# Three small edits to the edges of a TensorE-bound kernel: the order of the last products, 256-column matmuls in the first set, and the place of the branch hints

## The chip, the cores and the metric

One core of a Trainium2 chip. The time is the device time of one execution in microseconds (us). A trace was taken of one execution of each kernel; every other execution has only its time and its span.

Engine names: PE is TensorE's matmuls, PEld its weight loads, DVE VectorE, ACT ScalarE, POOL GpSimd, SP SyncE; SPq is DMA issue on SyncE. L250 is a line of the kernel of that run.

## The reference

```python
# x: 16 x 256 x 512, w1: 512 x 4096, w2: 2048 x 512, all float32
h = x @ w1
gate, value = np.split(h, 2, axis=-1)
h = np.maximum(gate, 0) * value
out = (h @ w2).astype(np.float32)
```

## The kernel before

Both matrix products are done with a seven-product scheme on 2x2 blocks (P1 to P7 instead of eight products), in float16, over four sets of 1024 rows. A first matmul runs through blocks of 128 hidden units (class `Block`, 128x512 outputs); a second one through four "pairs" of row blocks for each set (class `Pair`, 128x256 outputs). Each product of a pair ends in a small operation on ScalarE or VectorE and, in some cases, in a send of the output by SyncE.

The order of the products of the last set's second matmul is a list; the number is that of the pair:

```python
ORDER = ("P1 0, P1 1, P2 0, P2 1, P1 2, P5 0, P2 2, P6 0, P3 0, P7 0, P5 1, P6 1, P3 1, P7 1, P4 0, P5 2, P4 1, "
         "P6 2, P3 2, P7 2, P1 3, P4 2, P5 3, P2 3, P6 3, P3 3, P7 3, P4 3")
...
LAST_ORDER = ORDER.replace("P5 3, P2 3, P6 3, P3 3, P7 3", "P2 3, P6 3, P5 3, P7 3, P3 3")
# so it ends: P7 2, P1 3, P4 2, P2 3, P6 3, P5 3, P7 3, P3 3, P4 3
```

P6, P7 and P4 of a pair add into the same PSUM tile `Y`, and VectorE reads `Y` after P7 and before P4:

```python
def P7(self):
    nc.vector.scalar_tensor_tensor(out=self.o[:, 1, DO // 2:], in0=self.Y, scalar=1 / GS, in1=self.pu[:, 0],
                                   op0=MULT, op1=ADD)
    if self.end:
        self.send(1, slice(DO // 2, DO))

def P4(self):
    nc.scalar.activation(self.o[:, 1, :DO // 2], self.Y, COPY, scale=1 / GS)
    self.send(1, slice(0, DO // 2 if self.end else DO))
```

The scheme needs inputs of ordinary size, so the kernel checks its inputs while it works. A branch at the end leads to a plain general way if the check failed, and over it (some 3,360 TensorE instructions) if not. Hints for that branch are placed by one job of the last second matmul:

```python
with tc.If(unfit > 0, label="general"):
    ...            # general_way: not run with these inputs
...
job(84, lambda: tc.mark_branch_hint_location("general", "LikelyTaken", [ENG.PE, ENG.DVE, ENG.SP]))
```

Although this job is traced near the end, the built program has the three hint instructions at the very start of TensorE's, VectorE's and SyncE's programs. In the trace they start at 0.82, 0.77 and 0.74 us and take 0.05 to 0.06 us each.

Of the kernel before, what the change touches and what calls it, by code (L numbers as in the profile page):

```python
# [9 lines left out]
F32, F32R, F16 = dt.float32, dt.float32r, dt.float16  # L10
# [4 lines left out]
ENG = mybir.EngineType  # L15

P = 128
TH = 512
# [8 lines left out]
@with_exitstack  # L27
def kernel(ctx: ExitStack, tc: tile.TileContext, x, w1, w2, out):






    nc = tc.nc
    x2 = x.flatten_outer_dims()
    out2 = out.flatten_outer_dims()
    flagpool = ctx.enter_context(tc.tile_pool(name="flagpool", bufs=1))
    flag = flagpool.tile([1, 1], dt.int32, name="flag")
    with ExitStack() as fast:  # L40
        unfit = fast_way(fast, tc, x2, w1, w2, out2, flag)
    with tc.If(unfit > 0, label="general"):
        with ExitStack() as general:
            general_way(general, tc, x2, w1, w2, out2)
# [52 lines left out]
def fast_way(ctx, tc, x2, w1, w2, out2, flag):  # L97
# [9 lines left out]
    nc = tc.nc  # L107
    T, D = x2.shape
    _, J = w1.shape
    H, DO = w2.shape  # L110
    NS = T // (2 * TH)
    NJ = H // P
    NB = 2 * TH // P

    ctx.enter_context(tc.manual_schedule(engines={ENG.PE, ENG.DVE, ENG.Activation, ENG.Pool, ENG.SP}))
    wpool = ctx.enter_context(tc.tile_pool(name="wpool", bufs=1))
    xpool = ctx.enter_context(tc.tile_pool(name="xpool", bufs=2))
    gpool = ctx.enter_context(tc.tile_pool(name="gpool", bufs=1))
# [2 lines left out]
    tmp = ctx.enter_context(tc.tile_pool(name="tmp", bufs=6))  # L121
# [9 lines left out]
    wop = {n: wpool.tile([P, 2, H], F16, name=f"w_{n}") for n in ("B11", "B21", "B22", "T1", "T2", "T3", "T4")}  # L131
# [26 lines left out]
    def x_tiles():  # L158

        o = {n: xpool.tile([P, 2, TH], F16, name=f"x_{n}", tag=f"x_{n}")  # L160
             for n in ("A11", "A12", "A22", "S1", "S2", "S3", "S4")}
        o["A21"] = o["S3"]
        return o
# [3 lines left out]
    def sum_of(o, n, eng=nc.vector):  # L167
        i0, i1, op = SUMS_X[n]
        eng.tensor_tensor(o[n], o[i0], o[i1], op=op)  # L169

    def sums_of(o, eng=nc.vector):
        for n in SUMS_X:
            yield sum_of(o, n, eng)
# [67 lines left out]
          "P5": ("T1", "S1"), "P6": ("T2", "S2"), "P7": ("T3", "S3")}  # L241

    class Block:
        def __init__(self, xo, g, jb):
            self.xo, self.g, self.jb, self.behind = xo, g, jb, ()

        def mm(self, name, ps, fresh):
            wn, xn = WX[name]
            for b in range(2):
                nc.tensor.matmul(ps, wop[wn][:, b, self.jb * P:(self.jb + 1) * P], self.xo[xn][:, b, :],  # L250
                                 start=fresh and b == 0, stop=b == 1, skip_group_check=True)

        def P1(self):
            self.X = psx.tile([P, TH], F32, name="X", tag="X")
# [11 lines left out]
        def P2(self):  # L266
            self.mm("P2", self.X, False)
# [17 lines left out]
        def P7(self):  # L285
            self.mm("P7", self.Y, False)
            nc.vector.scalar_tensor_tensor(out=self.c22, in0=self.Y, scalar=GS, in1=self.p5, op0=MULT, op1=ADD)  # L287
            for job in self.behind:
                job()
            second_halves()  # L290
# [13 lines left out]
    def second_halves():  # L304

        while later:
            later.pop(0).second_half()
# [34 lines left out]

    class Pair:
        def __init__(self, s, g, t):
            self.s, self.t = s, t
            self.end = s == NS - 1 and t != NB // 2 - 2
            o = {f"A{h + 1}{u + 1}": g[:, u * NJ // 2:(u + 1) * NJ // 2, h * TH + t * P:h * TH + (t + 1) * P]
                 for h in range(2) for u in range(2)}
            o.update({f"S{n + 1}": s_place[:, t % 2, n] for n in range(4)})
            self.op = o  # L350

        def product(self, name):
# [8 lines left out]
            for i in range(NJ // 2):  # L361
# [4 lines left out]
                if i % 2:  # L366
                    yield

        def send(self, h, c):
            nc.sync.dma_start(out=out_v[self.s, h, self.t, :, c], in_=self.o[:, h, c])  # L370

# [8 lines left out]
                some_look()  # L380

        def P2(self):
            self.o = tmp.tile([P, 2, DO], F32, name="o", tag="tmp")
            nc.scalar.activation(self.o[:, 0, :DO // 2], self.X, COPY, scale=1 / GS)
            if self.end:
                self.send(0, slice(0, DO // 2))
# [9 lines left out]
            self.send(0, slice(DO // 2 if self.end else 0, DO))  # L396

        def P7(self):
            nc.vector.scalar_tensor_tensor(out=self.o[:, 1, DO // 2:], in0=self.Y, scalar=1 / GS, in1=self.pu[:, 0],
                                           op0=MULT, op1=ADD)  # L400
            if self.end:
# [5 lines that stand above are left out]
            if self.t in ((0, 2) if self.s else (0, 1, 2)):  # L407
                some_look()

    ORDER = ("P1 0, P1 1, P2 0, P2 1, P1 2, P5 0, P2 2, P6 0, P3 0, P7 0, P5 1, P6 1, P3 1, P7 1, P4 0, P5 2, P4 1, "  # L410
             "P6 2, P3 2, P7 2, P1 3, P4 2, P5 3, P2 3, P6 3, P3 3, P7 3, P4 3")
    FIRST_ORDER = ("P1 0, P1 1, P2 0, P2 1, P1 2, P5 0, P2 2, P6 0, P3 0, P5 1, P6 1, P3 1, P5 2, P6 2, P3 2, P7 0, P7 1, "
                   "P4 0, P7 2, P4 1, P1 3, P4 2, P5 3, P2 3, P6 3, P3 3, P7 3, P4 3")
    LAST_ORDER = ORDER.replace("P5 3, P2 3, P6 3, P3 3, P7 3", "P2 3, P6 3, P5 3, P7 3, P3 3")

    def mm2_stream(s, pairs):
        for step in (LAST_ORDER if s == NS - 1 else ORDER if s else FIRST_ORDER).split(", "):
            name, t = step.split()
            yield from pairs[int(t)].product(name)
# [3 lines left out]
    def advance(stream, n, todo={}):  # L423

        for _ in range(n):
            if stream is None:
                return
            at = stream_at[stream] = stream_at.get(stream, -1) + 1
            for job in todo.get(at, ()):
                job()  # L430
            next(stream, 0)
# [45 lines left out]
    g = g_set[0]  # L477
    x_nat = x2.rearrange("(s h b p) d -> s h b p d", h=2, b=4, p=P)
    place = [*x_tiles().values()][:7] + [halfs.tile([P, 8, P], F16, name="xh", tag="xh")]
    xn = [[t.rearrange("p a b -> p (a b)").bitcast(F32) for t in place[4 * h:4 * h + 4]] for h in range(2)]  # L480
# [3 lines left out]
    half, other = (0, TH // 2), (TH // 2, TH)  # L484
# [42 lines left out]
    xo = x_tiles()  # L527
# [53 lines left out]
    sums = [{n: t[:, :, slice(*c)] for n, t in xo.items()} for c in (half, other)]  # L581
# [54 lines left out]
    def judge():  # L636
        n = st.shape[1]
        ok = wpool.tile([P, n], F32, name="ok")
        fit = wpool.tile([P, 2], F16, name="fit")
        nc.vector.tensor_scalar(out=ok, in0=st, scalar1=HIGH, scalar2=None, op0=LE)  # L640
        nc.vector.scalar_tensor_tensor(out=ok, in0=st, scalar=LOW, in1=ok, op0=GE, op1=MULT)
        nc.vector.memset(fit, 1.0)
        with nc.allow_low_precision("whole numbers below 2048"):
            nc.vector.tensor_reduce(out=fit[:, :1], in_=ok, axis=mybir.AxisListType.X, op=ADD)
        return fit

    def count(fit):
        n = P * st.shape[1]
        ps = psx.tile([P, TH], F32, name="X", tag="X")
        nc.tensor.matmul(ps[:1, :1], fit[:, :1], fit[:, 1:], start=True, stop=True)  # L650
        nc.vector.tensor_scalar(out=flag, in0=ps[:1, :1], scalar1=n - 0.5, scalar2=None, op0=LT)
# [14 lines left out]
    for s in range(NS):  # L666
        if s not in g_set:
            g_set[s] = gpool.tile([P, NJ, 2 * TH], F16, name="g", tag="g")
        g = g_set[s]
        first = NPLAIN if s == 0 else 0  # L670
        blocks = {jb: Block(xo, g, jb) for jb in range(first, NJ)}
        plan = {jb * PERIOD + at: (jb, n) for jb in blocks for n, at in SLOT.items()}
        if s == 0:
            for n in ("P5", "P2", "P3"):
# [6 lines left out]
        last = NJ * PERIOD  # L681
        todo = 3
        for at in range(first * PERIOD, (NJ - 1) * PERIOD + 14):
            if at == last - 7:
                pairs = [Pair(s, g, t) for t in range(NB // 2)]
                stream = mm2_stream(s, pairs)
            if at in plan:
                jb, n = plan[at]
# [17 lines left out]
                if s and n == "P3" and jb in SUMS and s + 1 < NS:  # L706
                    if jb == SUMS[0]:
                        sums = sums_of(xo_next, nc.gpsimd)
# [18 lines left out]
        def job(at, *what):  # L727
            jobs.setdefault(at, []).extend(what)

        for t, at in enumerate(SUMS_AT if s else SUMS_FIRST):  # L730
            sums = sums_of(pairs[t].op)
            for u in at:
                job(u, lambda sums=sums: next(sums))
        if s == 0:
# [6 lines left out]
        if s + 1 < NS:  # L741
            xo = xo_next
            if s == 0:
                sums = sums_of(xo)
                for u in (84, 90):
                    job(u, lambda sums=sums: next(sums))
            looks = [lambda i=i: LOOK_JOBS[i]() for i in range(8 * s, 8 * s + 8)]
            advance(stream, 112 - TAIL - 10, jobs)
            if s == 0:
                next(sums)  # L750
                next(sums)
        else:
            verdict = []
            job(18, lambda: verdict.append(judge()))
            job(46, lambda: count(verdict[0]))
            job(78, lambda: verdict.append(nc.values_load(
                flag[0:1, 0:1], min_val=0, max_val=1, skip_runtime_bounds_check_because="a comparison wrote it")))
            job(84, lambda: tc.mark_branch_hint_location("general", "LikelyTaken", [ENG.PE, ENG.DVE, ENG.SP]))
            advance(stream, 112, jobs)
        prev = stream  # L760
    return verdict[-1]
# [28 lines left out]
```

## Time and profile before

| | before |
|---|---|
| time, median of the three runs known when the prediction was made | 308.57 us |
| span of the traced execution | 307.16 us |
| PE busy | 301.6 us, 98% |
| first matmul's wait, and the last wait on loads | 1.3 us; up to 18.7 us |
| start of the last matmul to the end ("the tail" below) | 4.40 us |

From the page of the kernel before: the span, the first of the busy times (us, share of the span, instructions), and the start of its part 4, the chain of work that ended last.

```profile
span 307.2 us, 5283 instructions
...
PE 301.6 (98%) x1905; PEld 184.2 (60%) x1905; DVE 236.0 (77%) x388; ACT 176.3 (57%) x348; POOL 151.2 (49%) x189
...
PE 96%; DMA 2%; SPq 1%; issue 0%; ACT 0%
```

With PE at 98% and 96% of the chain, only the first and the last few microseconds can hold time that isn't a matmul. The timeline of the first microseconds of the kernel before (start us, duration us, engine, line, operation, output<-input, count; in brackets the idle time before it and what ended it):

```profile
0.85 0.87 SPq L488 DMA_DIRECT2D x_A<-in_x_dram  x2
...
8.25 0.42 PEld L498 LDWEIGHTS X<-ident,x_A 128*128 128x128 f32 x4 [0.37 <-DMA x_A<-in_x_dram]
...
18.66 0.11 PEld L250 LDWEIGHTS <-w_T 128*128 128x128 f16 x2 [0.52 <-POOL w_T L232]
```

The first x block is issued at 0.85 us, TensorE waits for the third at 8.25 us, and waits a last time at 18.66 us, for GpSimd's weight sums, which wait for loads too (2.5 us in one wait). After that there is no gap to speak of until the end: in the records no two matmuls from there on start more than 0.26 us apart, and the step of a 128x512 one is 0.216.

The timeline of the last microseconds of the kernel before:

```profile
301.39 0.42 DVE L399 SCALAR_TENSOR_TENSOR o<-Y,pu 128x256 f32<-128x256 f32 x1 [3.56 <-PE Y L362]
...
301.99 1.04 PE L362 MATMUL Y<-v_T,g 128*128 128x256 f16 x8
302.20 0.42 DVE L394 SCALAR_TENSOR_TENSOR o<-W,pu 128x256 f32<-128x256 f32 x1 [0.38 <-PE W L362]
303.07 0.38 ACT L405 ACTIVATE o<-Y 128x256 f32<-128x256 f32 x1 [2.24 <-PE Y L362]
```

VectorE reads P7's result from 301.39 to 301.81, TensorE's last product P4 begins at 301.99, ScalarE copies it by 303.45, and the last send follows. The timeline of SyncE alone from 303.4 us on has this one row:

```profile
303.48 1.34 SPq L370 DMA_DIRECT2D out_dram<-o  x1
```

The issue of this 128 KB send takes 1.34 us, where 8 of the 12 issues of that size in this trace take 0.33. The DMA view of the same stretch (303.1 us to the end: queue, kind, packets, MB, share of the 16 engines; then the issue, with us to landing):

```profile
q8 instruction: 1, 0.02, 2.0%
q14 instruction: 1, 0.01, 0.6%
issues: line engine op xcount, KB each, median us to landing
out_dram<-o SPq DMA_DIRECT2D x1, 128.0 KB, 2.7
```

The send lands 2.7 us after its issue began. Beside it one packet of 16 KB on queue q8 and one of 8 KB on q14 are instruction fetches. The records give their times: q8 from 303.15 to 304.44 us, 1.26 us after TensorE's branch at 301.89.

### The profile page before, as it was taken

What the parts mean: (1) busy time and instruction counts of PE and PEld (TensorE: products, weight loads), DVE (VectorE), ACT (ScalarE), POOL (GpSimd) and SP (SyncE); (2) the same over time, 40 slices, a digit from 0 to 9 for tenths busy, and PEclk for the clock granted to TensorE, in tenths of its full rate; (3) what the DMA queues carried; (4) which work ended last, traced back from release to release, by engine and by line L of the source; (5) the groups of instructions that cost most, each with busy time, mean ns of one, the idle gap of its engine ahead of it and who ended that gap; (6) DMA issues with size and microseconds to landing.
All of it is one profiled execution on the core that took longest, in us unless ns stands there. A gap on an engine that the chain in (4) does not pass through costs nothing.

```text
span 307.2 us, 5283 instructions
## 1 busy us (share of the span) xinstructions
PE 301.6 (98%) x1905; PEld 184.2 (60%) x1905; DVE 236.0 (77%) x388; ACT 176.3 (57%) x348; POOL 151.2 (49%) x189
## 2 busy tenths in 40 slices
PE   8999999999999999999999999999999999999994
PEld 7744444588844444478864444458884444447883
DVE  2579888899778888887538888888536888888851
ACT  2488896455865555537855555546866555553231
POOL 2389999800068999300029889700007988700000
PEclk9999999999999999999999999999999999999999
DMA  6985779965775270001354910000325110001132
GB/s 204 358 259 179 239 171 176 229 123 80 260 209 88 69 137 3 0 0 55 136 182 108 207 34 2 0 2 9 130 101 174 35 34 0 3 1 34 54 106 87
DMA packets 35836, 32.87 MB, mean 107 GB/s; under 512 B 14432, under 2 KB 31328, under 8 KB 35680
## 3 DMA queue, kind: packets, MB, share of 16 engines
q1 hardware_dynamic: 33536, 26.22, 28.3%
q0 software_dynamic: 2272, 6.29, 11.4%
q8 instruction: 16, 0.26, 0.4%
q14 instruction: 12, 0.10, 0.1%
HBM read 27.26 MB, written 12.58 MB: 130 GB/s over the span
## 4 chain that ended last, share of the span: by engine, by line
PE 96%; DMA 2%; SPq 1%; issue 0%; ACT 0%
PE Y L250 26%; PE X L250 17%; PE W L250 17%; PE Y L362 14%; PE W L362 9%; PE X L362 9%; DMA x_A<-in_x_dram 2%; PE X L325 1%; PE W L325 1%; PE Y L325 1%; PE Y L498 0%; PE X L498 0%; SPq L217 0%; SPq L488 0%; ACT o L405 0%
## 5 line engine op out<-in xcount | busy, mean ns | idle before, releaser
L250 PEld LDWEIGHTS <-w_T 128*128 128x128 f16 x496 | 48.3, 98 | 57.3 <-POOL w_T L232 1.1
L179 POOL TENSOR_TENSOR fold<-xh 128x1024 f32<-128x1024 f16 x16 | 30.3, 1894 | 94.6 <-DMA xh<-x 93.7
L250 PE MATMUL X<-x_A,w_B 128*128 128x512 f16 x248 | 73.8, 379 | 0.0
L250 PE MATMUL Y<-x_S,w_T 128*128 128x512 f16 x220 | 65.5, 379 | 0.0
L250 PEld LDWEIGHTS <-w_B 128*128 128x128 f16 x372 | 36.3, 98 | 42.1
L277 DVE SCALAR_TENSOR_TENSOR cc<-W,pu 128x512 f32<-128x512 f32 x62 | 42.9, 691 | 21.1 <-ACT pu L271 21.1
L257 ACT COPY Y<-X 128x512 f32<-128x512 f32 x62 | 35.4, 571 | 38.2 <-PE X L250 37.9
L271 ACT ACTIVATE pu<-Y 128x512 f32<-128x512 f32 x62 | 37.1, 598 | 33.9 <-PE Y L250 33.0
L182 POOL TENSOR_TENSOR fold<-fold 128x512 f32<-128x512 f32 (+2 forms) x96 | 51.8, 539 | 7.5
L362 PEld LDWEIGHTS <-w_stage 128*128 128x128 f16 x512 | 50.0, 98 | 5.9
L287 DVE SCALAR_TENSOR_TENSOR cc<-Y,pu 128x512 f32<-128x512 f32 x62 | 42.9, 691 | 6.7
L282 DVE SCALAR_TENSOR_TENSOR g<-X,cc 128x512 f16<-128x512 f32 x62 | 42.8, 691 | 2.3
L299 DVE SCALAR_TENSOR_TENSOR g<-Y,cc 128x512 f16<-128x512 f32 x62 | 42.2, 681 | 1.8 <-PE Y L250 1.8
L362 PEld LDWEIGHTS <-g 128*128 128x128 f16 x384 | 37.5, 98 | 8.2
L264 ACT ACTIVATE pu<-W 128x512 f32<-128x512 f32 x62 | 37.2, 600 | 0.8 <-PE W L250 0.6
L250 PE MATMUL W<-x_S,w_B 128*128 128x512 f16 x124 | 36.9, 379 | 0.0
L250 PE MATMUL W<-x_S,w_T 128*128 128x512 f16 x124 | 36.9, 379 | 0.0
L250 PE MATMUL Y<-x_A,w_T 128*128 128x512 f16 x124 | 36.9, 379 | 0.0
L362 PE MATMUL X<-w,g 128*128 128x256 f16 x256 | 31.9, 273 | 0.0
L394 DVE SCALAR_TENSOR_TENSOR o<-W,pu 128x256 f32<-128x256 f32 x16 | 6.8, 423 | 19.4 <-PE W L362 19.4
L169 DVE TENSOR_TENSOR w_stage<-g 128x1024 f16<-128x1024 f16 x32 | 21.4, 684 | 0.2
L232 POOL TENSOR_TENSOR w_T<-w_stage 128x512 f16<-128x512 f32 (+1 forms) x16 | 18.7, 1173 | 2.5 <-DMA w_stage<-in_w_dram 2.5
(100 smaller groups left out, 307.5 us busy)
## 6 DMA issues: line engine op xcount, KB each, us to landing
w_stage<-in_w_dram SPq DMA_DIRECT2D x14, 512.0 KB, 6.0
out_dram<-o SPq DMA_DIRECT2D x26, 256.0 KB, 2.1
x<-in_x_dram POOLq DMA_DIRECT2D x4, 1024.0 KB, 9.1
xh<-x SPq DMA_DIRECT2D x16, 256.0 KB, 3.0
w<-in_w_dram POOLq DMA_DIRECT2D x2, 1024.0 KB, 10.2
out_dram<-o SPq DMA_DIRECT2D x12, 128.0 KB, 1.7
w_stage<-in_w_dram SPq DMA_DIRECT2D x4, 256.0 KB, 5.4
x_S<-in_x_dram SPq DMA_DIRECT2D x4, 256.0 KB, 6.5
```

The costliest lines, as they stand in the source:

```text
L169: eng.tensor_tensor(o[n], o[i0], o[i1], op=op)
L179: nc.gpsimd.tensor_tensor(fold, t, t, op=MULT)
L182: nc.gpsimd.tensor_tensor(fold[:, :, :m], fold[:, :, :m], fold[:, :, m:2 * m], op=ADD)
L250: nc.tensor.matmul(ps, wop[wn][:, b, self.jb * P:(self.jb + 1) * P], self.xo[xn][:, b, :], start=fresh and b == 0, stop=b == 1, skip_group ...
L257: nc.scalar.copy(out=self.Y, in_=self.X)
L264: nc.scalar.activation(self.p5, self.W, COPY, scale=GS)
L271: nc.scalar.activation(self.u2, self.Y, COPY, scale=GS)
L277: nc.vector.scalar_tensor_tensor(out=self.c12, in0=self.W, scalar=GS, in1=self.u2, op0=MULT, op1=ADD)
L282: nc.vector.scalar_tensor_tensor(out=self.g[:, self.jb, :TH], in0=self.X, scalar=0.0, in1=self.c12, op0=MAX, op1=MULT)
L287: nc.vector.scalar_tensor_tensor(out=self.c22, in0=self.Y, scalar=GS, in1=self.p5, op0=MULT, op1=ADD)
L299: nc.vector.scalar_tensor_tensor(out=self.g[:, self.jb, TH:], in0=self.Y, scalar=0.0, in1=self.c22, op0=MAX, op1=MULT)
L362: nc.tensor.matmul(ps, self.op[an][:, i], vop[wn][:, i], start=name in ("P1", "P5") and i == 0, stop=i == NJ // 2 - 1, skip_group_check=True)
```

## The change

Intent, as far as the edits show it: take the hints away from the start of the programs, give SyncE none, move P7 of the last pair away from the end, and split one product of the first set into two halves of columns.

```diff
+    def in_order():
+        order.enter_context(tc.manual_schedule(engines={ENG.PE, ENG.DVE, ENG.Activation, ENG.Pool, ENG.SP}))
...
         def mm(self, name, ps, fresh):
             wn, xn = WX[name]
-            for b in range(2):
-                nc.tensor.matmul(ps, wop[wn][:, b, self.jb * P:(self.jb + 1) * P], self.xo[xn][:, b, :],
-                                 start=fresh and b == 0, stop=b == 1, skip_group_check=True)
+            for c in (half, other) if name in self.in_halves else ((0, TH),):
+                for b in range(2):
+                    nc.tensor.matmul(ps[:, slice(*c)], wop[wn][:, b, self.jb * P:(self.jb + 1) * P],
+                                     self.xo[xn][:, b, slice(*c)], start=fresh and b == c[0] == 0, stop=b == 1,
+                                     skip_group_check=True)
...
-    LAST_ORDER = ORDER.replace("P5 3, P2 3, P6 3, P3 3, P7 3", "P2 3, P6 3, P5 3, P7 3, P3 3")
+    LAST_ORDER = ORDER.replace("P7 2, P1 3, P4 2, P5 3, P2 3, P6 3, P3 3, P7 3",
+                               "P1 3, P7 2, P6 3, P5 3, P7 3, P4 2, P2 3, P3 3")
...
+    def hint_here():
+        order.close()
+        traced = nc.cur_bb.bb.instructions
+        n = len(traced)
+        tc.mark_branch_hint_location("general", "LikelyTaken", [ENG.PE, ENG.DVE])
+        for i in nc.cur_bb.bb.instructions[n:]:
+            last = next(x for x in reversed(traced[:n]) if x.engine == i.engine and "Tile" not in type(x).__name__)
+            tc.add_manual_dep(i, last.name, ...)     # the hint stays where it was traced
+        in_order()
...
-        blocks = {jb: Block(xo, g, jb) for jb in range(first, NJ)}
+        blocks = {jb: Block(xo, g, jb, () if s else ("P5",)) for jb in range(first, NJ)}
...
+            if s == NS - 1 and t == 3:
+                sums = (sum_of(pairs[3].op, n) for n in ("S1", "S2", "S3", "S4"))
...
-            job(84, lambda: tc.mark_branch_hint_location("general", "LikelyTaken", [ENG.PE, ENG.DVE, ENG.SP]))
+            job(40, hint_here)
```

(The output tile `o` is now made by whichever of P2 and P7 comes first.) The new order ends P1 3, P7 2, P6 3, P5 3, P7 3, P4 2, P2 3, P3 3, P4 3.

In the built programs TensorE's hint is now instruction 3591 and its branch 3883 (before: 5 and 3827); VectorE's hint is 484 and its branch 503 (before: 5 and 503); SyncE has none.

More of the change, by code (lines that the diff above doesn't have):

```diff
@@ L113, in fast_way @@
     NB = 2 * TH // P
-    ctx.enter_context(tc.manual_schedule(engines={ENG.PE, ENG.DVE, ENG.Activation, ENG.Pool, ENG.SP}))
+    order = ctx.enter_context(ExitStack())
+    def in_order():
+        order.enter_context(tc.manual_schedule(engines={ENG.PE, ENG.DVE, ENG.Activation, ENG.Pool, ENG.SP}))
+    in_order()
     wpool = ctx.enter_context(tc.tile_pool(name="wpool", bufs=1))
@@ L243, in fast_way, with __init__ @@
     class Block:
-        def __init__(self, xo, g, jb):
-            self.xo, self.g, self.jb, self.behind = xo, g, jb, ()
+        def __init__(self, xo, g, jb, in_halves=()):
+            self.xo, self.g, self.jb, self.behind, self.in_halves = xo, g, jb, (), in_halves
         def mm(self, name, ps, fresh):
             wn, xn = WX[name]
-            for b in range(2):
-                nc.tensor.matmul(ps, wop[wn][:, b, self.jb * P:(self.jb + 1) * P], self.xo[xn][:, b, :],
-                                 start=fresh and b == 0, stop=b == 1, skip_group_check=True)
+            for c in (half, other) if name in self.in_halves else ((0, TH),):
[3 more added lines that the diff above has]
+                                     skip_group_check=True)
         def P1(self):
@@ L344, in __init__ @@
         def __init__(self, s, g, t):
-            self.s, self.t = s, t
+            self.s, self.t, self.o = s, t, None
             self.end = s == NS - 1 and t != NB // 2 - 2
@@ L367, in product, with outputs @@
                     yield
+        def outputs(self):
+            if self.o is None:
+                self.o = tmp.tile([P, 2, DO], F32, name="o", tag="tmp")
         def send(self, h, c):
@@ L382, in P2 @@
         def P2(self):
-            self.o = tmp.tile([P, 2, DO], F32, name="o", tag="tmp")
+            self.outputs()
             nc.scalar.activation(self.o[:, 0, :DO // 2], self.X, COPY, scale=1 / GS)
@@ L398, in P7 @@
         def P7(self):
+            self.outputs()
             nc.vector.scalar_tensor_tensor(out=self.o[:, 1, DO // 2:], in0=self.Y, scalar=1 / GS, in1=self.pu[:, 0],
@@ L645, in judge @@
         return fit
+    def hint_here():
[5 more added lines that the diff above has]
+            last = next(x for x in reversed(traced[:n]) if x.engine == i.engine and "Tile" not in type(x).__name__)
+            tc.add_manual_dep(i, last.name, mybir.DependencyInfo(mybir.DependencyClass.NoSync, mybir.DependencyReason.DATA),
+                              reason="the hint stays where it was traced")
+        in_order()
     def count(fit):
```

## The prediction

> **What bounds the kernel.** TensorE. The page gives PE 301.6 us busy of a 307.2 us span (98%), granted clock 0.999; the chain of waits is 96% PE. In the timeline, PE has no idle stretch after 18.7 us. A 128x512 product starts every 216 ns and a 128x256 one every 109 ns. Three things can move: the data-bound start (to 18.7 us, where PE waits for x, w_stage and POOL's w_T), the matmuls, and the 4.1 us tail after the last matmul (303.03 to 307.16).
>
> **The tail, from the timeline and records.** Last matmul ends 303.03; ACT copies P4's output 303.07-303.45; SyncE issues the last 128 KB send at 303.478; it lands at 306.19; SyncE closes. That send's issue took 1344 ns and it landed after 2.72 us; undisturbed sends of that size (287.3, 301.8) took 332 ns and 1.69 us. A 16 KB instruction fetch (queue q8) runs at 303.15-304.44, 1.26 us after PE's branch. The fetch at 298.45 met a send likewise (issue 1041 ns, landing 2.48 us). So about 1.03 us of the tail (2.72-1.69) looks like the fetch's doing. [...]
>
> **What the change does.**
> 1. Hints. In before they stand first in PE's, DVE's and SyncE's programs, although traced late. In after PE's stands about 290 instructions ahead of the branch, DVE's a dozen; SyncE has none. SyncE's hint took 0.74-0.85 us, directly ahead of the first x load, so the data-bound start should come about 0.11 us earlier. On the critical path.
> 2. P5 in halves: 14 blocks, each 4x109 instead of 2x216 ns: +5 ns each, +0.07 us, on the critical path. It also adds 56 PE instructions, shifting where fetches fall: that at 298.45 should come about 3 us earlier (56 at 18.3 per us)[...].
> 3. P7 ahead. The last two products (P3, P4) and their sends stay. P7's send leaves the tail, P2's takes its place, and pair 2's 256 KB send moves from 298.2 to about 300.9. P7's read of Y left P4 only about 0.1 us of slack; afterwards over 1.5. PE did not visibly stall there, so worth 0 to 0.05 us. New deadlines (second pair-3 sum done about 296.3, needed 296.75) hold.
>
> **Sum.** Without a change in the fetch at the branch: 308.57-0.11+0.07-0.02, about 308.5. If it goes, or comes when no send is pending, another 1.0 less: 307.5. Hint and shift aim there[...]. I give each half.
>
> **Predicted: 308.0 us, 8 in 10 between 307.3 and 308.7.** Chances: faster by over 2% 0.01, within 2% 0.98, slower 0.01.
>
> **What would show it.** First x load issued near 0.74 us instead of 0.85; 28 more matmuls, PE still without gaps; PE's last matmul at or within 0.1 us of 303.0; the last send's issue near 332 ns and landing 1.7 us (fetch gone) or near 1.3 and 2.7 (fetch stays). Near 307.5 only if the former.
>
> **What would make it wrong.** Late pair-3 sums stalling PE by tenths; the 256 KB send delaying the last ones; DVE's hint too near its branch, giving a new fetch stall in the tail; a fetch hitting early loads.

The sum: about 308.5 us without a change in the fetch at the branch and 307.5 if it goes; half each gives 308.0.

## The result and the profile after

Ratios are the mean time of one kernel's runs over that of the other's of the same rounds, so not quite the ratio of the medians quoted. Most of the experiments' ratios come out when the traced execution is left out on both sides, which matters for e1.

The changed kernel took 308.00 us (median of 6, 307.41 to 308.67) against 308.54 (308.28 to 308.84) of the kernel before: ratio 0.9985, 95% interval 0.9971 to 1.0000. With a second run of the unaltered changed kernel (below) the means are 308.12 us (11 executions) and 308.56 us (39): 0.43 us, or 0.14%, gained. That is small, but it is where the prediction put it. The traces say where it can come from.

From the page of the changed kernel:

```profile
span 305.6 us, 5338 instructions
...
PE 300.7 (98%) x1933; PEld 187.0 (61%) x1933; DVE 236.0 (77%) x388; ACT 176.5 (58%) x348; POOL 151.2 (49%) x189
...
PE 96%; DMA 1%; SPq 0%; POOL 0%; ACT 0%; issue 0%
```

28 matmuls more, as predicted, and nothing else about the bound has changed. The traced execution was the fastest of the eleven (307.41 us), and that of the kernel before (308.93 us) was slower than all six of its result, so the two spans aren't typical. The timeline of its first microseconds:

```profile
0.74 0.87 SPq L501 DMA_DIRECT2D x_A<-in_x_dram  x2
...
17.68 0.11 PEld L256 LDWEIGHTS <-w_T 128*128 128x128 f16 x2 [0.31 <-POOL w_T L237]
```

The first x block is issued 0.11 us earlier, as predicted. But the last wait on loads ends 0.98 us earlier, not 0.11. The timeline of its last microseconds:

```profile
298.73 0.42 DVE L411 SCALAR_TENSOR_TENSOR o<-Y,pu 128x256 f32<-128x256 f32 x1 [1.67 <-PE Y L369]
...
300.20 1.04 PE L369 MATMUL W<-w,w_stage 128*128 128x256 f16 x8
...
301.08 1.04 PE L369 MATMUL Y<-v_T,g 128*128 128x256 f16 x8
301.28 0.42 DVE L405 SCALAR_TENSOR_TENSOR o<-W,pu 128x256 f32<-128x256 f32 x1 [2.12 <-PE W L369]
302.15 0.38 ACT L417 ACTIVATE o<-Y 128x256 f32<-128x256 f32 x1 [1.36 <-PE Y L369]
```

VectorE's read of P7's result (the first line) now ends at 299.15 us, 1.9 us before P4's first matmul. SyncE's row from 302.5 us on, and the DMA view from there to the end:

```profile
302.56 0.67 SPq L381 DMA_DIRECT2D out_dram<-o  x1
```

```profile
q14 instruction: 1, 0.01, 1.1%
issues: line engine op xcount, KB each, median us to landing
out_dram<-o SPq DMA_DIRECT2D x1, 128.0 KB, 2.1
```

The last send now takes 0.67 us to issue and lands after 2.1 us. The 16 KB fetch hasn't gone: the records have it on q8 at 301.92 to 302.86 us, so it begins before this window. The DMA view from 301.9 us on has it:

```profile
q8 instruction: 1, 0.02, 1.6%
```

It comes earlier against the last product: 0.08 us after the last matmul's start, where it came 0.39 us after it in the kernel before. TensorE's branch came 1.83 us ahead of the last matmul's start, instead of 0.87 us.

So the span of these two traces differs by 1.52 us: 0.96 us in the start, 0.60 in the tail, and 0.04 lost in the matmuls between. The times differ by 0.43 us on the mean. One trace of each isn't enough to share this out, hence the runs below.

### The profile page after: what moved, and what is told of

Read it like the earlier page. It is cut to its first block, busy times and chain, and to the rows that moved or that the text cites. A ratio compares the mean times of both kernels' runs of the same rounds, so it can differ in the third digit from the quotient of the medians.

```text
span 305.6 us, 5338 instructions
## 1 busy us (share of the span) xinstructions
PE 300.7 (98%) x1933; PEld 187.0 (61%) x1933; DVE 236.0 (77%) x388; ACT 176.5 (58%) x348; POOL 151.2 (49%) x189
## 4 chain that ended last, share of the span: by engine, by line
PE 96%; DMA 1%; SPq 0%; POOL 0%; ACT 0%; issue 0%
PE Y L256 26%; PE W L256 18%; PE X L256 18%; PE Y L369 14%; PE X L369 9%; PE W L369 9%; DMA w_stage<-in_w_dram 1%; PE W L332 1%; PE X L332 1%; PE Y L332 1%; PE Y L511 0%; PE X L511 0%; SPq L501 0%; POOL w_T L479 0%; SPq L222 0%; ACT o L417 0%
## 5 line engine op out<-in xcount | busy, mean ns | idle before, releaser
L256 PEld LDWEIGHTS <-w_T 128*128 128x128 f16 x524 | 51.1, 98 | 54.6 <-POOL w_T L237 0.9
L256 PE MATMUL W<-x_S,w_T 128*128 128x512 f16 (+1 forms) x152 | 36.9, 340 | 0.0
```

The lines of the kernel that those rows point to most:

```text
L256: nc.tensor.matmul(ps[:, slice(*c)], wop[wn][:, b, self.jb * P:(self.jb + 1) * P], self.xo[xn][:, b, slice(*c)], start=fresh and b == c[0] ...
```

## The experiments

Twelve kernels ran. E1 to e4 and e5, e10 to e12 ran on one chip, number 7, e6 to e9 on another, number 10; for the result's own two traces the record names no chip. Each ratio compares with the kernel before. The table holds what the traces show. "Start" is the time of VectorE's 21st scalar_tensor_tensor, about 32 us in, when the waits on loads are over. "Lead" is how far TensorE's branch comes ahead of the last matmul's start. "Fetch" is the 16 KB fetch after the branch: when it starts and ends, counted from the last matmul's start. "Issue" and "land" are of the last send, in us from its issue's start; that issue comes 0.72 us after the last matmul's start in every trace but one (0.80 without hints). "Tail" runs from the last matmul's start to the end.

| kernel | start | lead | fetch | issue | land | tail |
|---|---|---|---|---|---|---|
| before | 32.37 | 0.87 | +0.39 to +1.68 | 1.34 | 2.72 | 4.40 |
| before, again (e11) | 31.96 | 0.87 | +0.45 to +1.50 | 1.17 | 2.53 | 4.21 |
| halves alone (e2) | 32.25 | 0.87 | +0.47 to +1.41 | 0.33 | 2.19 | 3.87 |
| hints alone (e3) | 31.84 | 0.87 | +0.48 to +1.45 | 0.33 | 2.23 | 3.91 |
| before, near branch (e4) | 32.12 | 0.87 | none | 0.34 | 1.71 | 3.39 |
| order alone (e1) | 33.62 | 1.84 | -0.16 to +1.18 | 0.83 | 2.28 | 3.96 |
| order alone, again (e12) | 32.47 | 1.84 | -0.01 to +1.09 | 0.75 | 2.19 | 3.87 |
| changed | 31.41 | 1.83 | +0.08 to +1.02 | 0.67 | 2.12 | 3.80 |
| changed, again (e9) | 31.97 | 1.83 | +0.08 to +1.02 | 0.67 | 2.12 | 3.80 |
| VectorE's hint first (e6) | 31.81 | 1.84 | +0.08 to +1.01 | 0.67 | 2.11 | 3.79 |
| without halves (e8) | 32.05 | 1.83 | -0.13 to +1.04 | 0.58 | 2.03 | 3.71 |
| without hints (e7) | 31.68 | 1.84 | -0.82 to +0.54, and a second | 0.42 | 2.00 | 3.76 |
| no halves, VectorE's hint first (e10) | 31.72 | 1.84 | -0.14 to +1.12 | 0.77 | 2.23 | 3.91 |
| changed, near branch (e5) | 31.44 | 1.84 | -0.05 to +0.83 | 0.48 | 1.97 | 3.65 |

From the start mark to the last matmul's start every trace with whole P5 took 270.39 or 270.40 us, and every one with halves 270.43 or 270.44. The middle of the kernel doesn't vary. All that varies lies in the first 32 us and in the tail.

The theories. A: the fetch that follows TensorE's branch delays the last send; the new order lets TensorE reach the branch earlier, so the fetch is over sooner. B: the gain is all in the start, from the hints. C: the last send is slow for another reason than the fetch. D: the 4.40 us tail of the kernel before was one bad trace.

### e1: the order alone

```diff
 # on the kernel before
-    LAST_ORDER = ORDER.replace("P5 3, P2 3, P6 3, P3 3, P7 3", "P2 3, P6 3, P5 3, P7 3, P3 3")
+    LAST_ORDER = ORDER.replace("P7 2, P1 3, P4 2, P5 3, P2 3, P6 3, P3 3, P7 3",
+                               "P1 3, P7 2, P6 3, P5 3, P7 3, P4 2, P2 3, P3 3")
+    # and the last pair's sums in the order S1 to S4; o made by P2 or P7
```

Expected:

> The kernel before with the order of the last second matmul alone changed (P7 of the last pair four products ahead, its sums in the order S1 to S4); hints and P5 as before. Theory A (fetch timing): PE's sequencer was held by the wait of the last product, P4, on VectorE's read of P7, so its branch came 0.87 us ahead of the last matmul's start; freed, the branch comes about 1.8 us ahead of it as in the changed kernel, the 16 KB fetch starts at about the last matmul's start instead of 0.4 us after it, the last send's issue falls from 1344 ns to about 670 ns and its landing from 2.72 to about 2.1 us: span 0.5 to 0.7 us shorter, time about 308.0. Rival B (the gain is all in the start, from the hint): no gain here, 308.5, last send's issue still near 1.3 us.

Measured: 307.96 us median (307.54 to 309.74), ratio 0.9978 (0.9965 to 0.9991). With the traced execution all six have a mean of 308.23 us against 308.53 in the same rounds, 0.9990. The branch's lead went from 0.87 to 1.84 us and the tail was 3.96 us. The traced execution was the slowest of the six, with a start 1.1 us later than any other.

What follows: the order alone moves the branch, and with it the fetch, as theory A says. The fetch doesn't keep a fixed distance from the branch, though: with a hint and a fetch it begins 1.26 to 1.35 us after the branch in the four traces with the old order and 1.67 to 1.92 us after it in those with the new. So 0.96 us of lead became 0.3 to 0.6 us of earlier fetch; why isn't shown. Whether the order also brings the whole gain was left to a second run (e12).

### e2: the halves alone

```diff
 # on the kernel before, with the changed mm()
-        blocks = {jb: Block(xo, g, jb) for jb in range(first, NJ)}
+        blocks = {jb: Block(xo, g, jb, () if s else ("P5",)) for jb in range(first, NJ)}
```

Expected:

> The kernel before with P5 of the first set in column halves alone. As a cost of matmuls alone: +0.07 us, 308.6. Padding theory: the 56 added instructions move the last sequential fetch about 3 us earlier (298.4 to 295.4 us) and the send beside it lands in 1.7 us, but the fetch after the branch stays 1.26 us after it and the last send's issue stays near 1.3 us: no gain, 308.6. Rival: [...]last send's issue 332 ns, time about 307.5.

Measured: 308.25 us median (307.86 to 308.77), ratio 0.9993 (0.9980 to 1.0006). Middle 0.04 us longer. The fetch stayed and came 1.35 us after the branch, but the issue of the last send took 0.33 us, not the 1.3 expected, and it landed after 2.19 us; tail 3.87.

What follows: splitting costs what the matmuls say (0.04 us) and takes no fetch away, though the rival expected that. The expectation of the issue missed: a fetch under way doesn't always stretch the issue. Where it doesn't, the landing comes 1.86 us after the issue's end, instead of 1.37 us as in the undisturbed send of e4. The records count a send's completion in 16 steps. In e4 they come 1.52 to 1.71 us after the issue's start; here 14 come by 1.69 us and the last two at 2.06 and 2.19 us, and in e3 14 by 1.68 us and the last two at 1.78 and 2.23 us. So a small part of the send is late. In the traces with a stretched issue all 16 are late together (the first at 1.61 to 2.53 us).

### e3: the hints alone

```diff
 # on the kernel before, with the changed hint_here()
-            job(84, lambda: tc.mark_branch_hint_location("general", "LikelyTaken", [ENG.PE, ENG.DVE, ENG.SP]))
+            job(40, hint_here)
```

Expected:

> The kernel before with the hints alone moved (PE's and VectorE's into the last second matmul, SyncE's taken away). Theory A: first x load issued 0.11 us earlier (0.74 us), start and time 0.1 us shorter, 308.4; the last send's issue still near 1.3 us. VectorE's event after its branch comes about 3 us after the branch instead of 0.6 us, as in the changed kernel[...]; harmless here since the last send lands later. Rival B (the start gains 0.9 us, as in the one profiled run of the changed kernel): time 307.6 to 307.8.

Measured: 308.13 us median (307.84 to 309.05), ratio 0.9996 (0.9981 to 1.0011). First x load issued at 0.74 us. VectorE's event after its branch came at 304.80 us, 3.1 us after the branch (before: 0.63 us), still 0.4 us ahead of the last landing. The last send's issue took 0.33 us against the 1.3 expected, and the tail 3.91.

What follows: the time alone tells neither A nor B. VectorE's part came as expected.

### e4: the kernel before with a near branch

```diff
 # on the kernel before; right for these inputs alone
         with ExitStack() as general:
-            general_way(general, tc, x2, w1, w2, out2)
+            nc.gpsimd.memset(general.enter_context(tc.tile_pool(name="g_w", bufs=1)).tile([P, 1], F32, name="g_t"), 0.0)
```

Expected:

> The kernel before with the unused general way cut to one memset on GpSimd, so that PE's and VectorE's branch at the end goes only a few instructions ahead (right for this data alone, where the general way is never taken). Nothing else changes. Theory A: no 16 KB fetch after PE's branch, last send's issue about 332 ns and landing about 1.7 us after it: span about 1.0 us shorter, time about 307.5. Rival C (the last send is slow because it is the last, or for the writes before it): issue stays near 1.3 us and time 308.5.

Measured: 307.84 us median (307.43 to 309.25), ratio 0.9986 (0.9967 to 1.0005; one execution of 309.25 us widens it). The last send in this trace's timeline, and the DMA view from 303.1 us to the end:

```profile
303.23 0.34 SPq L370 DMA_DIRECT2D out_dram<-o  x1
```

```profile
q1 hardware_dynamic: 288, 0.26, 27.6%
issues: line engine op xcount, KB each, median us to landing
out_dram<-o SPq DMA_DIRECT2D x1, 128.0 KB, 1.7
```

There is no instruction queue in the stretch, the issue takes 0.34 us, and the send lands after 1.7 us. The tail is 3.39 us, the shortest of all.

What follows: theory C falls for the trace. With the same order, the same sends and a start between those of the kernel before's two traces (32.12 us), taking the fetch away takes 0.8 to 1.0 us off this send and 0.8 to 1.0 us off the tail. The edit also takes away the 8 KB fetch on q14 at the end and the 16 KB fetch at 298.45 us; their share isn't separated, but in e5 a 16 KB fetch without one on q14 still makes the landing 1.97 us. In e2 and e3 one or two of the 16 steps come late while a packet of 16 KB takes 0.93 to 0.97 us; which DMA engine carried the packet isn't in the trace, so how it makes them late isn't shown. Nor is it shown why the issue itself is stretched in the others. In ten of the thirteen traces with a fetch, the issue of the last send ends 0.25 to 0.38 us after the end of the fetch. (The others are e2 and e3, where the landing is late instead, and the one without hints, whose first fetch ended earlier.) That speaks against theory C too, and so does a send that isn't the last: in the kernel before, the one issued at 299.11 us took 1.04 us, and its issue ended 0.37 us after the fetch of 298.45 to 299.79 us.

### e9: the changed kernel again

No edit. Expected:

> The changed kernel unaltered, for a second trace and more times beside the three runs that follow. Theory A: the tail from the last matmul's start to the end is again 3.7 to 4.0 us (one trace so far: 3.80; before: 4.40), branch of PE 1.83 us ahead of the last matmul's start, time 308.0 to 308.1. Rival D (the 4.40 us of the kernel before was one bad trace, the tails are alike, and only the start differs from run to run): tails scatter between 3.8 and 4.4 whatever the order of products.

Measured: 308.12 us median (307.98 to 308.48), ratio 0.9990 (0.9977 to 1.0003). Tail 3.80, the same as in the first trace; start 31.97 us, 0.56 us later than in the first. The first trace's start was a lucky one. The tail wasn't.

### e6: VectorE's hint back at the start

```diff
 # on the changed kernel
-        tc.mark_branch_hint_location("general", "LikelyTaken", [ENG.PE, ENG.DVE])
+        tc.mark_branch_hint_location("general", "LikelyTaken", [ENG.PE])
...
             job(40, hint_here)
+            job(84, lambda: tc.mark_branch_hint_location("general", "LikelyTaken", [ENG.DVE]))   # lands at the start
```

Expected:

> The changed kernel with VectorE's hint alone back at the start of its program. Theory A: VectorE's event after its branch comes about 0.6 us after the branch instead of 3.0 us, with one fetch on its queue instead of two; SyncE's wait for VectorE (263 ns in the changed kernel's trace) goes, but the last send's landing still ends the tail: 0 to 0.1 us gained, time within 0.1 us of the changed kernel's. Rival E (VectorE's late event holds the end in most executions): 0.2 us or more gained.

Measured: 307.87 us median (307.56 to 308.62), ratio 0.9984 (0.9971 to 0.9998). VectorE's event came 0.63 us after its branch instead of 3.07 (e9), with one fetch of 8 KB on q14 after the branches instead of two. The tail stayed at 3.79.

What follows: the changed kernel's hint for VectorE, 19 instructions ahead of the branch, doesn't do its work (without any hint, in e7, the event comes 3.01 us after the branch); at the start of the program it did (0.63 us). Why isn't shown. It isn't late in time: it runs 15.0 us ahead of VectorE's branch, and TensorE's hint, which works (its branch took 0.41 us in the first trace of the changed kernel, 3.63 us in e7), 15.1 us ahead of TensorE's. The 2.4 us are hidden behind the last send's landing (in that first trace the event comes at 304.26 us, the landing at 304.67). Against e9 the means differ by 0.15 us (308.02 and 308.17), with scatters as wide as that; no gain is shown.

### e8: the changed kernel without the halves

```diff
 # on the changed kernel
-        blocks = {jb: Block(xo, g, jb, () if s else ("P5",)) for jb in range(first, NJ)}
+        blocks = {jb: Block(xo, g, jb, ()) for jb in range(first, NJ)}
```

Expected:

> The changed kernel with the first set's P5 back in whole products. Matmul cost theory: PE 0.07 us shorter, time within 0.1 us of the changed kernel's (308.0). Padding theory (the 56 instructions place a fetch favourably): last sequential fetch at about 298 us instead of 295, which meets the sends near the end; 0.2 us or more slower than the changed kernel.

Measured: 307.94 us median (307.69 to 308.41), ratio 0.9982 (0.9970 to 0.9995). Middle 0.04 us shorter, tail 3.71 instead of 3.80; the last sequential fetch came at 299.15 us instead of 295.54. Not slower.

What follows: nothing here speaks for the halves. No favourable placing of fetches is to be seen.

### e7: the changed kernel without hints

```diff
 # on the changed kernel
-            job(40, hint_here)
```

Expected:

> The changed kernel without any hint. Theory A[...]: PE's and VectorE's first event after their branches now waits for a fetch, PE's by 1 to 3 us after the branch, VectorE's by about 3 us as before; two large fetches after PE's branch; as PE branches 1.8 us ahead of its last matmul, the end is held by 0 to 1 us: time 308.0 to 309.0. Rival (hints do nothing): PE's events as in the changed kernel, one large fetch.

Measured: 308.04 us median (307.60 to 309.56), ratio 0.9992 (0.9973 to 1.0011). The DMA view from 301 us to the end:

```profile
q8 instruction: 2, 0.03, 3.4%
q14 instruction: 2, 0.02, 0.9%
```

Two 16 KB fetches instead of one, and TensorE's branch took 3.63 us in the records (0.4 to 0.96 us in all traces with a hint and a far branch). Its next instruction came at 303.98 us, 3.7 us after the branch began and still 0.94 us ahead of the last landing at 304.92. Tail 3.76.

What follows: TensorE's hint does something, and it works at the start of the program (the branch took 0.50 us in the kernel before) as well as 292 instructions ahead of the branch (0.41 us in the changed kernel). But with the new order the branch comes so early, 1.84 us ahead of the last matmul's start, that even one of 3.63 us hides behind the last send. How the hint works isn't shown: in the changed kernel's trace TensorE's hint runs at 284.94 us, and the next 16 KB packet on q8 comes at 294.95.

### e11: the kernel before against itself

No edit. Expected:

> The kernel before, unaltered, against itself: the ratio should be 1 with an interval that holds it, which shows what a ratio of these runs is worth. Its second trace decides on the tail: theory A' (order of products and place of the fetch both matter) expects 3.9 to 4.4 us from the last matmul's start to the end, last send landing 2.2 to 2.7 us after its issue, PE's branch 0.87 us ahead of the last matmul. Theory D (the 4.40 us was one bad trace) expects 3.85 to 3.95, as in the two other kernels with the old order of products (3.87 and 3.91), in which case the new order is worth only about 0.1 us of tail.

Measured: 308.59 us median (308.34 to 308.97), ratio 1.0003 (0.9987 to 1.0018). Tail 4.21, issue 1.17 us, landing 2.53 us.

What follows: two traces of the kernel before have tails of 4.40 and 4.21, so theory D falls in its strict form. All eight traces with the new order and a far branch lie between 3.71 and 3.96 (mean 3.83), the four with the old order between 3.87 and 4.40 (mean 4.10): 0.27 us on the mean. But the ranges overlap, and four of the eight ran on chip 10, where no trace has the old order. On chip 7 alone the means are 3.91 (e1, e12, e10) and 4.00 (e11, e2, e3), 0.08 us apart. And e10 on chip 7 has a tail 0.20 us longer than e8 on chip 10; the two differ in VectorE's hint alone, which made no difference to the tail in e6. So how much of the tail is due to the order isn't settled. What doesn't overlap is the end of the fetch, on chip 7 alone either: +1.41 us or later with the old order, +1.18 us or earlier with the new (the second fetch of e7 left out).

### e12: the order alone, again

The edit of e1. Expected:

> The kernel of the first experiment (new order of products alone) again, since its profiled execution was its slowest (309.74 us, a late start) and the rest averaged 307.9. If the order alone brings the gain (theory A): mean 307.9 to 308.1, ratio 0.998, tail 3.7 to 3.96. If the other runs were luck (theory D): mean 308.3 to 308.5, ratio above 0.999.

Measured: 308.49 us median (308.05 to 308.68), ratio 0.9992 (0.9976 to 1.0008). Tail 3.87.

What follows: by its times this run sides with the rival's expectation, by its trace with theory A. With e1 the twelve executions have a mean of 308.30 us, 0.26 us below the 308.56 of the kernel before. They run from 307.54 to 309.74 us, so that this mean is good to about 0.35 us at best (an estimate from their scatter): taken together they don't show a gain of the order alone. The 0.6 us that e1 seemed to bring was in part luck.

### e5: the changed kernel with a near branch

The edit of e4 on the changed kernel. Expected:

> The changed kernel with the unused general way cut to one memset, so no far branch (right for this data alone). Theory A: no fetch after the branches, last send's issue 332 ns and landing 1.7 us, VectorE's event within 0.6 us of its branch, tail 3.4 us instead of 3.8: time about 0.4 us below the changed kernel's, 307.6. If only the order of products mattered for the tail, nothing more is left to gain: 308.0.

Measured: 307.67 us median (307.31 to 308.10), ratio 0.9974 (0.9958 to 0.9989). The expectation was half missed: one 16 KB fetch was still there, 0.05 us before the last matmul's start, though the branch was near; it ended earlier (+0.83), and the landing took 1.97 us instead of 1.7, the tail 3.65 instead of 3.4. VectorE's next instruction came 0.25 us after its branch.

What follows: the time is the best of all and the direction fits theory A, but the edit didn't remove what it was meant to. Why this near branch fetched and that of e4 didn't isn't shown.

### e10: without the halves and with VectorE's hint first

The edits of e6 and e8 together. Expected:

> The changed kernel without the halves and with VectorE's hint first: the new order of products, PE's hint in the last second matmul, none for SyncE. If the parts add up: 0.07 us (halves) and 0 to 0.1 us (VectorE) below the changed kernel, 307.9, ratio to before 0.998; not to be told from the changed kernel by these times, only by the trace (28 matmuls fewer, VectorE's event 0.6 us after its branch).

Measured: 308.79 us median (307.78 to 309.44), ratio 1.0007 (0.9989 to 1.0024). In the trace, whose execution was the fastest of the six (307.78 us), all is as expected: start 31.72, middle 270.39, VectorE's event 0.63 us after its branch, tail 3.91. The other five took 308.1 to 309.4 us.

What follows: a miss, and not explained. Its two edits alone did no harm, and the one trace shows none. Two or three tenths of a microsecond can't be told apart by six executions, and here not even half a microsecond is safe. No version that beats the changed kernel is shown.

## Why the prediction was right or wrong

The time and the range were right (308.0 predicted, 308.0 measured), but partly by a sum of errors. Point by point:

- **What bounds the kernel** held: 98% PE and 96% of the chain in both pages. That only the start, the matmuls and the tail can move was borne out sharply: the stretch from the start mark to the last matmul is the same to 0.01 us in all kernels with the same matmuls.
- **The fetch slows the last send** held: the reading of 1.03 us from 2.72 less 1.69 was answered by e4, where the landing is 1.71 us.
- **"If it goes [...] I give each half"** was a fork, and neither branch came. The fetch stayed, but came 0.3 to 0.6 us earlier against the last matmul. The issue took 0.67 us, between the 332 ns and the 1.3 us that were to mark the two outcomes.
- **P7 ahead, "worth 0 to 0.05 us"** left out a path. I looked for a stall of TensorE's matmuls and found none, rightly. What I missed is that P7's read may have held up what comes after P4 in TensorE's program. In all five traces with the old order VectorE's read of P7 ends 0.94 us ahead of the last matmul's start, the branch follows 0.07 us later, and the eight matmuls of P4 are still to start. In all nine with the new order the branch leads by 1.83 or 1.84 us, the read ends 2.69 us ahead, and 17 matmuls are still to start at the branch. That the wait is the cause is read from this coincidence; no run lifted the wait alone. What the path is worth isn't settled: the mean tails differ by 0.27 us over all traces, by 0.08 us on chip 7 alone.
- **Hints, "about 0.11 us earlier"**: the first load's issue came exactly so (0.85 to 0.74; SyncE's hint had run at 0.74). The start as a whole was mis-sized: the six traces with SyncE's hint have a median of 32.31 us, the eight without 31.76, so 0.55 us. The ranges barely touch (31.96 to 33.62, 31.41 to 32.05), and on chip 7 alone they don't (31.96 to 33.62, 31.44 to 31.84). No run takes SyncE's hint alone away. VectorE's hint isn't behind it: e6 and e10 have it first and start at 31.81 and 31.72. How 0.11 us of issue becomes 0.5 us isn't shown. It isn't fully borne out by the times either: e3, with the hints alone, has a mean of 308.31 us, 0.25 below the kernel before, with an interval that holds none.
- **Halves, "+0.07 us"** was right as far as it can be seen: the middle is 0.04 to 0.05 us longer. Only eight of the 14 split products lie after the start mark, so that is 5 to 6 ns each, where 5 were predicted. The notion that they place the fetches well isn't supported (e2, e8).
- **PE's last matmul "within 0.1 us of 303.0"** failed: it ended at 302.11 us in the first trace and 302.67 in the second, because of the start.
- **"DVE's hint too near its branch"**: the stall named as a risk came (3.0 us) and cost nothing that shows. That nearness is its cause isn't shown.

The terms of the traces, 0.27 (tail) and 0.55 (start) less 0.04, add up to 0.78 us, and the times show 0.43. With the terms of chip 7 alone (0.08, and 0.53 for the start) the sum would be 0.57. The traces are one execution each, and starts scatter by half a microsecond; the difference stays open.

## What to carry to other kernels

When one engine is busy for 98% of the time, split the span into start, middle and end with a marker instruction in each trace: here the middle repeats to 0.01 us among kernels with the same matmuls, so what differs lies at the edges. One trace of an edge isn't enough: two traces of one kernel differed by up to 0.19 us in the tail (4.40 and 4.21) and by more than 1 us in the start (33.62 and 32.47). Look at what meets the last send: here a fetch of instructions did, and the tail was 0.8 to 1.0 us shorter where it was gone. Here a product that waited for a buffer seems to have held back what its engine had behind it, the branch at the end too: the branch came 0.07 us after the read that freed the buffer and 0.87 us ahead of the last matmul's start, and 1.83 or 1.84 us ahead of it once that read ended 2.69 us ahead (argued from where the branches come, not tested alone). With the last products ordered so that no such wait stands near the end, that fetch was over earlier, at most 1.18 us after the last matmul's start instead of 1.41 us or more, though it still met the last send. Before a hint is trusted, look at when the engine's first instruction after the branch comes: the same hint that works at the program's start (0.63 us from branch to event) did nothing visible 19 instructions ahead of the branch (2.88 to 3.11 us from branch to event in four traces, 3.01 us without a hint).
